# Latent queries projected in the first stage of a two-layer encoder kernel, and the latent values made beside the last band pair

## The chip, the cores and the metric

The kernel runs on one core of one Trainium2 chip. The metric is the device time of one launch in microseconds (us). TensorE (PE) does the matmuls, VectorE (DVE), ScalarE (ACT) and GpSimd (POOL) the rest, and SyncE (SP) issues nearly all transfers (DMAs).

## What is computed

Two layers of a streaming encoder, for 1024 prompt frames and 64 frames of a later chunk (1088 columns in all, with 256 cached positions). The first ("even") layer has two groups of eight heads beside each other: multi-head latent attention and chunk-band attention. The second layer is a stick-breaking attention. The change lies in the even layer alone:

```python
def _even_project(x, pos, w_in, g_q, w_uq, g_kv):
    h = x @ w_in
    q_a = (_rms_norm(h[..., :o1], g_q) @ w_uq).reshape(B, S, H_A, NOPE_DIM + ROPE_DIM)
    q_a = jnp.concatenate([q_a[..., :NOPE_DIM], _rope(q_a[..., NOPE_DIM:], pos)], -1)
    ckv = _rms_norm(h[..., o1:o2], g_kv)
    kr = _rope(h[..., o2:o3], pos)
    ...
def _mla_keys(ckv, kr, w_ukv):
    kv = (ckv @ w_ukv).reshape(B, T, H_A, NOPE_DIM + V_DIM)
    k = jnp.concatenate([kv[..., :NOPE_DIM], jnp.broadcast_to(kr[:, :, None, :], (B, T, H_A, ROPE_DIM))], -1)
    return k, kv[..., NOPE_DIM:]
def _even_prompt(x, pos, w_in, g_q, w_uq, g_kv, w_ukv, table, w_out):
    q_a, ckv, kr, q_b, k_b, v_b = _even_project(x, pos, w_in, g_q, w_uq, g_kv)
    k_a, v_a = _mla_keys(ckv, kr, w_ukv)
    o_a = _blockwise(lambda qb, pb: _softmax_attend(qb, k_a, v_a, _chunk_mask(pb, pos), MLA_SCALE), q_a, pos)
    o_b = _band_prompt(q_b, k_b, v_b, table)
    y = jnp.concatenate([o_a.reshape(B, S, H_A * V_DIM), o_b.reshape(B, S, H_B * HEAD_DIM)], -1) @ w_out
```

The query latent has 768 features, the key latent 256, and the rotated part of a query 32 features a head.

## The kernel before

All numbers are float32. A product is made from three matmuls: `split` (line 147) writes a high part H (ScalarE copies to a rounded type) and a low part L (VectorE subtracts), and `mm3` or `dense` (line 450) adds H.H, H.L and L.H in PSUM. PSUM has two buffers each of the tags d and s, three of t and one of pv.

The even layer runs in stages. `latents` (line 320) loads x and the weights and projects, tile by tile of 128 tokens, first the key latents (ck, and the rotated key kr), then the query latents; both are normed, transposed and stored raw to DRAM (`ck_d`, `krT_d`, `qn_d`). It also writes constant rows of the queries (qconst) to `qr_d`. Then `even_mixer` (line 745) works through four band pairs, two heads a pair: `proj` makes keys, queries and values of a pair, `attend` (line 729) its attention. For each row block: scores in PSUM, a maximum with the bias on VectorE (R, mx), exp on ScalarE, a reciprocal and a scaling on GpSimd, transposes on TensorE, a split of the transposed weights (wtH, wtL), the PV matmuls, and `put_output` (line 657), which folds two halves of the result (o; in latent attention through a second buffer, otmp, on GpSimd).

`paced` (line 558) spreads the steps of the next projection over the attention of the pair before, so the matmuls of the two are interleaved; the marks that it is given say behind which attention matmul a step may stand. Pairs 0 to 2 carry the projection of the next band pair in that way. Band pair 3 carries the query projection: `load_latents` (line 779) loads the query latents back from `qn_d` (six loads, 3.3 MB) and splits them, and does the same with ck; `rotate` (line 831, three chunks, weight blocks m = 4, 5) and `nope` (line 825, m = 0 to 3, three chunks each) project them and store the parts to `qr_d` and `qm_d`. What of it is not done when pair 3 ends runs behind it alone.

Then come the 11 value blocks (V, in two tiles of 6 and 2 heads), the latent keys of pair 0 (`proj_mla`, line 898, which also loads the queries of a pair from `qr_d` and `qm_d` and the weights w_mk), and four pairs of latent attention, each beside the keys of the next. Two key sets alternate; the constant rows of the second are copied from the first (k0H to k1L).

The order on each engine is that of the program after this pacing; a transfer waits in SP's queue for its buffer and for its place there, and each transfer takes one of eight completion lanes in turn, so it also waits until the eighth transfer before it has landed.

Of the kernel before, what the change touches and what calls it, by code (L numbers as in the profile page):

```python
# [7 lines left out]
F32 = mybir.dt.float32  # L8
# [111 lines left out]
class Net:  # L120
# [58 lines left out]
    def weight(self, src, shape, mark=None):  # L179
        nc = self.nc  # L180
# [4 lines left out]
        self.after(nc.sync.dma_start(tiles[0], src), mark)  # L185
# [134 lines left out]
    def latents(self):  # L320
        nc, io = self.nc, self.io
        pa = self.pool("pa", "right")
        wckH = self.tl(pa, [P, KD, LAT], "wckH", 1, F32R)
        wckL = self.tl(pa, [P, KD, LAT], "wckL", 1, F32R)
        wqlH = self.tl(pa, [P, KD, QL], "wqlH", 1, F32R)
        wqlL = self.tl(pa, [P, KD, QL], "wqlL", 1, F32R)

        def ck_piece(k):
            raw = self.tl(pa, [P, 2, LAT], "praw", 2)
            nc.sync.dma_start(raw, io["w_ck"][:, k : k + 2, :])  # L330
            self.split(wckH[:, k : k + 2, :], wckL[:, k : k + 2, :], raw)

        def ql_piece(k):
            raw = self.tl(pa, [P, QL], "praw", 2)
# [5 lines left out]
        def x_piece(t):  # L340
            t0, n = TOK[t]
            s = (slice(None), slice(None), slice(t0, t0 + n))
            raw = self.tl(pa, [P, KD, P], "xraw", 2)[:, :, :n]
# [28 lines left out]
        rope = self.tl(pa, [P, 9, ROPE], "rope", 1)  # L372
        nc.sync.dma_start(rope, io["rope_tok"])
        gkv = self.bcast(pa, io["g_kv"], CKV, "gkv")
        gq = None

        for t, (t0, n) in enumerate(TOK):
# [5 lines left out]
            sq = self.tl(pa, [P, 384], "sq", 2)  # L383
            ss = self.tl(pa, [P, 2], "ss", 3)
            nc.scalar.activation(sq[:n, :CKV], ps[:n, :CKV], AF.Square, accum_out=ss[:n, 0:1])
            kr = self.tl(pa, [P, ROPE], "kr", 2)
            nc.scalar.activation(kr[:n], ps[:n, CKV:LAT], AF.Copy)
            r = self.rstd(pa, ss[:n, 0:1], 1.0 / CKV, 1e-6, n)
            cat = self.tl(pa, [P, LAT], "cat", 2)
            nc.vector.scalar_tensor_tensor(cat[:n, :CKV], ps[:n, :CKV], r[:n], gkv[:n], op0=ALU.mult, op1=ALU.mult)  # L390
            cos, sin = rope[:n, t, :16], rope[:n, t, 16:]
            m = self.tl(pa, [P, 4, 16], "ropem", 2)
# [12 lines left out]
            stg = self.tl(pa, [P, 3, P], "stg", 3)  # L405
            nc.scalar.activation(stg[:, :2, :n], tp[:, :2, :n], AF.Copy)
            nc.scalar.activation(stg[:ROPE, 2, :n], tp[:ROPE, 2, :n], AF.Copy)
            nc.sync.dma_start(self.ck_d[:, :, t0 : t0 + n], stg[:, :2, :n])
            nc.sync.dma_start(self.krT_d[:, t0 : t0 + n], stg[:ROPE, 2, :n])

        gq = self.bcast(pa, io["g_q"], QL, "gq", marks[5])
        for t, (t0, n) in enumerate(TOK):
            if t == 4:
                first = self.weight(io["w_bk"][0], [P, KD, P], marks[-1])
            halves = []
            ss = self.tl(pa, [P, 2], "ss", 3)
            for h in range(2):
                ps = project(t, (wqlH, wqlL), h * 384, 384)
                sq = self.tl(pa, [P, 384], "sq", 2)
# [9 lines left out]
            for h in range(2):  # L429
# [4 lines left out]
                stg = self.tl(pa, [P, 3, P], "stg", 3)  # L434
                nc.scalar.activation(stg[:, :, :n], tp[:, :, :n], AF.Copy)
                nc.sync.dma_start(self.qn_d[:, 3 * h : 3 * h + 3, t0 : t0 + n], stg[:, :, :n])

        for c0, n in CHUNKS:
            qc = self.tl(pa, [ROPE, 384], "qc", 1)
            self.after(nc.sync.dma_start(qc[:, :n], io["qconst"][:, c0 : c0 + n]), marks[10])  # L440
            x = self.parts(pa, qc[:, :n], 2)
# [4 lines left out]
        pa.release()  # L446
        return first, marks[14]
# [209 lines left out]
    def put_output(self, cp, pv, width):  # L657
# [3 lines left out]
        if self.pool_fold:  # L661
            tmp = self.tl(self.pool_fold, [64, 256], "otmp", 2)
# [82 lines left out]
    def even_mixer(self):  # L745
# [30 lines left out]
        qnH = qnL = ckH = ckL = lc = kp0 = lq = up = None  # L776
        ksets = []

        def load_latents():


            nonlocal qnH, qnL, ckH, ckL, lc, kp0, lq, up
            X.release()
            lc = self.pool("lc", "left")
            kp0 = self.pool("kp0", "left")
            lq = self.pool("lq", "left")
            up = self.pool("uq", "left")
            qnH, qnL = (self.tl(lq, [P, KQ, T], tag, 1, F32R) for tag in ("qnH", "qnL"))
            ckH, ckL = (self.tl(lc, [P, 2, NK], tag, 1, F32R) for tag in ("ckH", "ckL"))

            def piece(H, L, src, n):
                raw = self.tl(up, [P, 2, 384], "raw", 3)
                nc.sync.dma_start(raw[:, :, :n], src)
                self.split(H, L, raw[:, :, :n])

            for c0, n in CHUNKS:
# [23 lines left out]
        def uq(ps, m, c0, n):  # L820
            if m not in uw:
                uw[m] = self.weight(io["w_uq"][m], [P, KQ, P])
# [937 lines left out]
```

## Time and profile before

| | |
|---|---|
| median of 3 runs | 2847.84 us (2845.25 to 2851.31) |
| profiled execution | 2850.05 us |
| its span on the core | 2848.3 us, 46969 instructions |
| mean granted clock of TensorE | 0.985 of full speed |

The span starts with the first instruction; the 1.75 us beside it in the execution's own time lie around it. The views read below are the page's header, windows (busy time of each engine in a stretch, with the clock granted to TensorE and the share and rate of the DMA engines), the chain of waits, which follows the work that ended last back from wait to wait, timelines and groups by form. `x12` is a count. An engine that waits for something is idle there, and the arrow names the releaser that came last.

### The profile page before, as it was taken

The page shows a single profiled execution, that of the slowest core. Times are in us where ns is not written, and L with a number is a line of the kernel's source. Part 1 is how long each engine was busy: PE and PEld are TensorE (multiplying, and loading weights), DVE is VectorE, ACT ScalarE, POOL GpSimd, SP SyncE. Part 2 cuts the span into 40 slices and gives each one's busy share as a digit, 9 for nine tenths or more (in the row PEclk, how much of TensorE's full clock was granted, in tenths as well). Part 3 has the DMA queues.
Part 4 walks back from the last instruction along what each step waited for, and adds up shares of the span by engine and source line. Part 5 has one row for each costly group of instructions (what it writes and reads, how often), then busy time and mean ns, then how long its engine had stood idle before and what let it go on. Part 6 is the DMA issues. An engine that isn't in the chain of part 4 may idle for free.

```text
span 2848.3 us, 46969 instructions
## 1 busy us (share of the span) xinstructions
PE 2742.8 (96%) x16907; PEld 2506.5 (88%) x16907; DVE 2158.1 (76%) x3822; ACT 1521.4 (53%) x3128; POOL 779.3 (27%) x891
## 2 busy tenths in 40 slices
PE   8999979999999999999999999999999999999998
PEld 7999978887899998878789999998879999977886
DVE  4256774885867777999967888888787777689998
ACT  4366654883555556333257777777445555543331
POOL 3223241662200002221543334344330000122235
PEclk9999999999999999999999999999999999999999
DMA  7322245334243447344321111112242444654432
GB/s 199 104 62 67 83 124 147 83 116 131 90 145 128 151 156 265 120 144 135 104 86 57 52 51 59 51 53 97 70 151 86 152 147 132 234 173 136 157 116 83
DMA packets 233320, 334.49 MB, mean 117 GB/s; under 512 B 45152, under 2 KB 165760, under 8 KB 233088
## 3 DMA queue, kind: packets, MB, share of 16 engines
q1 hardware_dynamic: 233088, 331.49, 37.1%
q8 instruction: 134, 2.20, 0.3%
q14 instruction: 98, 0.80, 0.1%
HBM read 216.72 MB, written 112.21 MB: 115 GB/s over the span
## 4 chain that ended last, share of the span: by engine, by line
PE 74%; DVE 10%; DMA 5%; ACT 5%; issue 3%; POOL 1%; SPq 1%; DVEq 0%; ACTq 0%; POOLq 0%
PE d L153 8%; PE d L154 8%; PE d L155 8%; PE t L153 5%; PE t L154 5%; PE t L155 5%; PE s L153 5%; PE s L155 5%; PE s L154 5%; PE t L171 4%; PE s L572 3%; PE pv L706 2%; PE pv L704 2%; PE pv L153 2%; PE pv L155 2%
## 5 line engine op out<-in xcount | busy, mean ns | idle before, releaser
L640 POOL TENSOR_TENSOR G<-G,S 128x384 f32<-128x384 f32 (+4 forms) x200 | 208.7, 1048 | 339.6 <-DVE S L637 139.8
L153 PE MATMUL d<-xH,wH 128*128 128x384 f32 (+1 forms) x792 | 266.4, 336 | 1.9 <-ACT kraw L539 1.4
L154 PE MATMUL d<-xL,wH 128*128 128x384 f32 (+1 forms) x792 | 264.3, 334 | 0.0
L155 PE MATMUL d<-xH,wL 128*128 128x384 f32 (+1 forms) x792 | 262.5, 331 | 0.0
L149 DVE TENSOR_TENSOR wtL<-t,wtH 128x512 fp32r<-128x512 f32 (+2 forms) x328 | 196.8, 618 | 46.9 <-ACT wtH L148 43.3
L148 ACT ACTIVATE wtH<-t 128x512 fp32r<-128x512 f32 (+2 forms) x328 | 170.3, 545 | 54.1 <-PE t L171 33.9
L148 ACT ACTIVATE wo<-wo 128x1024 fp32r<-128x1024 f32 (+4 forms) x109 | 96.1, 888 | 157.0 <-DMA wo<-a_d 27.1
L579 POOL TENSOR_TENSOR R<-R,inv 128x640 f32<-128x640 f32 (+6 forms) x100 | 120.4, 1212 | 199.7 <-DVE inv L578 87.5
L704 PE MATMUL pv<-wtH,V 128*128 128x256 f32 (+1 forms) x624 | 160.4, 281 | 8.5 <-ACT o L664 3.7
L706 PE MATMUL pv<-wtL,V 128*128 128x256 f32 (+1 forms) x624 | 156.8, 291 | 5.5 <-DVE wtL L149 5.3
L153 PEld LDWEIGHTS d<-xH,wH 128*128 128x128 f32 x792 | 149.7, 189 | 5.5 <-ACT kraw L539 2.2
L637 DVE TENSOR_TENSOR_SCAN S<-S,own 128x513 f32<-128x513 f32 (+3 forms) x144 | 144.2, 1010 | 11.4 <-ACT S L630 9.8
L154 PEld LDWEIGHTS d<-xL,wH 128*128 128x128 f32 x792 | 149.8, 189 | 1.2
L155 PEld LDWEIGHTS d<-xH,wL 128*128 128x128 f32 x792 | 149.7, 189 | 1.2
L704 PEld LDWEIGHTS pv<-wtH,V 128*128 128x128 f32 x624 | 120.7, 193 | 14.3 <-ACT o L664 6.3
L706 PEld LDWEIGHTS pv<-wtL,V 128*128 128x128 f32 x624 | 120.8, 194 | 8.9 <-DVE wtL L149 7.8
L171 PE MATMUL t<-ident,G 128*128 128x128 f32 x600 | 106.9, 282 | 14.3 <-POOL G L640 8.2
L572 PE MATMUL s<-kS,qH 128*128 128x384 f32 (+3 forms) x288 | 106.6, 373 | 6.9 <-DVE mx L595 4.1
L149 DVE TENSOR_TENSOR wo<-wo,wo 128x1024 fp32r<-128x1024 f32 (+4 forms) x80 | 92.9, 1165 | 21.9 <-ACT wo L148 20.9
L630 ACT ACTIVATE S<-s 128x384 f32<-128x384 f32 (+4 forms) x200 | 99.0, 495 | 12.6 <-PE s L572 9.1
L631 ACT ACTIVATE G<-s 128x384 f32<-128x384 f32 (+4 forms) x200 | 100.1, 500 | 0.0
L572 PE MATMUL s<-kS,qL 128*128 128x384 f32 (+3 forms) x288 | 97.8, 342 | 0.0
(1714 smaller groups left out, 9841.1 us busy)
## 6 DMA issues: line engine op xcount, KB each, us to landing
wo<-a_d SPq DMA_DIRECT2D x59, 512.0 KB, 3.8
wo<-in_w_dn SPq DMA_DIRECT2D x30, 512.0 KB, 5.5
a_d<-wo SPq DMA_DIRECT2D x27, 544.0 KB, 3.7
a_d<-sl SPq DMA_DIRECT2D x23, 544.0 KB, 4.0
sl<-in_w_up SPq DMA_DIRECT2D x22, 512.0 KB, 4.5
sl<-a_d SPq DMA_DIRECT2D x21, 512.0 KB, 3.8
sl<-in_w_dn SPq DMA_DIRECT2D x19, 512.0 KB, 5.3
xs<-a_d SPq DMA_DIRECT2D x19, 512.0 KB, 3.7
```

The costliest lines, as they stand in the source:

```text
L148: self.nc.scalar.activation(H, src, AF.Copy)
L149: (engine or self.nc.vector).tensor_tensor(L, src, H.bitcast(F32), op=ALU.subtract)
L153: i = mm(out, aH, bH, start=first, stop=False)
L154: mm(out, aH, bL, start=False, stop=False)
L155: mm(out, aL, bH, start=False, stop=last)
L171: return self.nc.tensor.transpose(out, in_, self.ident[:n, :n])
L572: self.nc.tensor.matmul(ps[:, :n], q, k, start=i == 0, stop=i == len(passes) - 1)
L579: nc.gpsimd.tensor_tensor(R[:, :nk], R[:, :nk], inv.to_broadcast([P, nk]), op=ALU.mult)
L637: nc.vector.tensor_tensor_scan(s[r], s[r], own, carry, op0=ALU.mult, op1=ALU.max)
L640: nc.gpsimd.tensor_tensor(G[:, :n], G[:, :n], S[:, 1 : n + 1], op=ALU.mult)
L704: mm(out, v, wH[:, s : s + n], start=bi == 0 and s == 0, stop=False)
L706: mm(out, v, wL[:, s - n : s], start=False, stop=bi == len(banks) - 1 and j == bank[-1][0])
```

## The change

The query latents are no longer stored: `latents` splits them into tiles in SBUF (`qn_parts`), and a new stage `queries` behind it projects and rotates them there and stores `qr_d` and `qm_d`; the qconst rows follow. The key latents are stored as H and L, and band pair 3 loads them so. w_mv and all four w_mk are loaded once, ahead of pair 3. The value blocks 0 to 7 are paced beside pair 3, and blocks 8 to 10 stand with the first latent keys; V is one tile of eight heads, whose last two are copied to a second tile by a transfer. The ring otmp has one buffer in place of two, and the ring of the staged ck tiles two in place of three.

```diff
@@ latents
-            stg = self.tl(pa, [P, 3, P], "stg", 3)
-            nc.scalar.activation(stg[:, :2, :n], tp[:, :2, :n], AF.Copy)
-            nc.scalar.activation(stg[:ROPE, 2, :n], tp[:ROPE, 2, :n], AF.Copy)
-            nc.sync.dma_start(self.ck_d[:, :, t0 : t0 + n], stg[:, :2, :n])
-            nc.sync.dma_start(self.krT_d[:, t0 : t0 + n], stg[:ROPE, 2, :n])
+            parts = [self.tl(pb, [P, 2, P], f"stg{x}", 2, F32R)[:, :, :n] for x in "HL"]
+            self.split(*parts, tp[:, :2, :n])
+            for i in range(2):
+                nc.sync.dma_start(self.ck_d[i, :, :, t0 : t0 + n], parts[i].bitcast(F32))
+            kr = self.tl(pb, [ROPE, P], "krT", 2)
...
+            if t in (2, 4):
+                uw[t // 2 + 3] = self.weight(io["w_uq"][t // 2 + 3], [P, KQ, P], marks[-1])
...
-                stg = self.tl(pa, [P, 3, P], "stg", 3)
-                nc.scalar.activation(stg[:, :, :n], tp[:, :, :n], AF.Copy)
-                nc.sync.dma_start(self.qn_d[:, 3 * h : 3 * h + 3, t0 : t0 + n], stg[:, :, :n])
+                c = slice(t0 - t // 3 * 384, t0 - t // 3 * 384 + n)
+                self.split(*(x[:, 3 * h : 3 * h + 3, c] for x in qn_parts[t // 3]), tp[:, :, :n])
+        pa.release()
+        late, first = self.queries(qn_parts, uw)
@@ queries (new; nope and rotate as before, on qn_parts)
+            ps = self.ps("ds")
+            first = uq(ps, m, c, n)
+            nc.sync.dma_start(self.qm_d[m, :, :, c0 : c0 + n], self.parts(up, ps[:, :n], 4))
...
+        for c in range(3):
+            rotate(c)
+        late = None
+        for m in range(4):
+            for c in range(3):
+                i = nope(m, c)
+                late = late or i
+            if m == 0:
+                first = self.weight(io["w_bk"][0], [P, KD, P], late)
@@ put_output
-            tmp = self.tl(self.pool_fold, [64, 256], "otmp", 2)
+            tmp = self.tl(self.pool_fold, [64, 256], "otmp", 1)
@@ load_latents
-            for c0, n in CHUNKS:
-                for k in range(0, KQ, 3):
...
-                    nc.sync.dma_start(raw, self.qn_d[s])
-                    self.split(qnH[s], qnL[s], raw, nc.gpsimd if c0 >= 768 else None)
+            for c0, n in ((0, 384), (384, 384), (768, 256), (SEQ, 64)):
+                kc = c0 if c0 < SEQ else SEQ + PAST
+                for i, x in enumerate((ckH, ckL)):
+                    nc.sync.dma_start(x[:, :, kc : kc + n].bitcast(F32), self.ck_d[i, :, :, c0 : c0 + n])
...
+            wv = self.weight(io["w_mv"], [P, 2, 512])
...
+            mk = self.weight([io["w_mk"][m] for m in range(4)], [P, KD, P])
@@ even_mixer
-        uqs = [lambda a=a: rotate(*a) for a in CHUNKS] + [lambda a=a: nope(*a) for a in ((m, c0, n) for m in range(4) for c0, n in CHUNKS)]
-        self.paced(uqs, marks[1:])
+        vals = [lambda j=j: values(j) for j in range(len(KEYBLK))]
+        self.paced(vals[:8], marks[1:])
...
-        Vs = [self.tl(vps[i], [P, 11, m, P], "V", 1, F32R) for i, m in enumerate((6, 2))]
...
-            w = self.weight(io["w_mk"][pair], [P, 2, P])
...
-        self.paced(steps, None)
+        self.paced(steps + vals[8:], None)
+        Vs.append(self.tl(vb, [P, 11, 2, P], "V", 1, F32R))
+        nc.sync.dma_start(Vs[1].bitcast(F32), Vs[0][:, :, 6:].bitcast(F32))
```

The order shows it at three places. On TensorE at the end of the last band pair, before: the last passes of the latent keys (d from ckH and the weight) stand ahead of the first latent scores (from k0H and q).

```order
L153 MATMUL d_5726<-ckH_4434,wH_1233_5698 128x512
L154 MATMUL d_5726<-ckL_4435,wH_1233_5698 128x512
L155 MATMUL d_5726<-ckH_4434,wL_1234_5699 128x512
L572 MATMUL d_5752<-k0H_4454,q_5705 128x384
L572 MATMUL d_5752<-k0L_4455,q_5705 128x384
L572 MATMUL d_5752<-k0H_4454,q_5705 128x384
L572 MATMUL s_5757<-k0H_4454,q_5705 128x512
```

After: the last PV passes of band pair 3 (pv) stand there instead.

```order
L774 MATMUL pv_5536<-wtH_5554,V_1939 128x256
L776 MATMUL pv_5536<-wtL_5555,V_1939 128x256
L774 MATMUL pv_5536<-wtH_5554,V_1939 128x128
L776 MATMUL pv_5536<-wtL_5555,V_1939 128x128
L642 MATMUL s_5736<-k0H_4985,q_5660 128x384
L642 MATMUL s_5736<-k0L_4986,q_5660 128x384
L642 MATMUL s_5736<-k0H_4985,q_5660 128x384
L642 MATMUL d_5741<-k0H_4985,q_5660 128x512
```

The latent keys and values have moved ahead of the last PV, and the first latent score has no matmuls between it and the band pair. On SP at the same place, before: the last of the four key copies (k1L) is followed by stores of the query projection (qm_d), two weight loads, more such stores and then the queries.

```order
L885 DMA k1L_5561<-k1L_4457 64x1344
L828 DMA qm_d<-raw_5365 256x1x384
L185 DMA wraw_5570<-in_w_mv 128x1024
L828 DMA qm_d<-raw_5388 256x1x320
L828 DMA qm_d<-raw_5417 256x1x384
L828 DMA qm_d<-raw_5440 256x1x384
L185 DMA wraw_5697<-in_w_mk 128x256
```

After: the copy of V, the key copies and the query loads (q, qS) stand close behind each other.

```order
L1063 DMA wH_2102_8409<-in_w_out 128x1024
L970 DMA V_5730<-V_5011 128x11x256
L779 DMA oT_d<-o_5430 64x256
L779 DMA oT_d<-o_5506 64x256
L932 DMA k0H_5650<-k0H_4985 64x1344
L932 DMA k0L_5651<-k0L_4986 64x1344
L779 DMA oT_d<-o_5562 64x256
L932 DMA k1H_5652<-k1H_4987 64x1344
L932 DMA k1L_5653<-k1L_4988 64x1344
L943 DMA q_5660<-qr_d 64x2x1024
L944 DMA qS_5658<-qr_d 64x2x64
L943 DMA q_5660<-qm_d 64x2x1024
```

Nothing of the query projection is left in between. On VectorE early in pair 3, before: splits of the loaded query latents (qnL) stand between the maxima (R, mx).

```order
L578 RECIPROCAL inv_4599<-sm_4597 128x1
L599 TENSOR_SCALAR nm_4629<-mx_4620 128x1
L149 TENSOR_TENSOR qnL_4433<-qnL_4433,qnH_4432 128x3x384 x2
L578 RECIPROCAL inv_4633<-sm_4631 128x1
L595 ISA R_4636,mx_4637<-s_4638,bias_4404 128x256
L595 ISA mx_4637 128x1
L149 TENSOR_TENSOR qnL_4433<-qnL_4433,qnH_4432 128x3x384
```

After: band values (V from t) and the first latent value block (V from d, 8 heads of 64) stand there.

```order
L149 TENSOR_TENSOR V_1939<-t_4929,V_1939 128x4x64
L648 RECIPROCAL inv_5036<-sm_5034 128x1
L669 TENSOR_SCALAR nm_5049<-mx_5040 128x1
L669 TENSOR_SCALAR nm_5104<-mx_5099 128x1
L149 TENSOR_TENSOR V_1939<-t_4929,V_1939 64x2x64
L149 TENSOR_TENSOR V_5011<-d_5566,V_5011 128x8x64
L665 ISA R_5111,mx_5112<-s_5113,bias_4942 128x256
L665 ISA mx_5112 128x1
```

The query latents' splits are gone from this stretch, and a value split has come in.

## Rows read from the trace of the kernel before

**Rows 1.** the page's busy times: us, share of the span, instructions of each engine.
```profile
PE 2742.8 (96%) x16907; PEld 2506.5 (88%) x16907; DVE 2158.1 (76%) x3822; ACT 1521.4 (53%) x3128; POOL 779.3 (27%) x891
```

**Rows 2.** windows of 20 us: PE, PEld, DVE, ACT, POOL busy; PEclk, DMA, GB/s.
```profile
200.00:220.00 20.00, 20.00 (x141) 19.80 (x140) 11.86 (x43) 13.64 (x35) 9.49 (x12) 1.00 0.26 76
...
380.00:400.00 20.00, 16.42 (x109) 15.81 (x109) 18.29 (x52) 10.58 (x25) 9.70 (x9) 0.88 0.32 79
400.00:420.00 20.00, 14.63 (x85) 13.51 (x85) 10.29 (x23) 8.66 (x20) 5.25 (x6) 0.91 0.34 100
...
480.00:500.00 20.00, 16.23 (x99) 15.10 (x100) 14.16 (x56) 12.34 (x30) 10.16 (x11) 0.83 0.07 16
500.00:520.00 20.00, 19.10 (x130) 17.27 (x130) 16.82 (x59) 17.15 (x41) 12.16 (x13) 1.00 0.65 148
```

**Rows 3.** chain of waits, 345 to 500 us: start, length, what.
```profile
351.93 9.69 DMA qnL<-qn_d
...
392.87 9.81 DMA qr_d<-raw
...
465.53 9.36 DMA q<-qm_d
474.94 6.57 DMA wraw<-in_w_mk
```

**Rows 4.** timeline of TensorE, 429 to 484 us: start, length, operation.
```profile
429.95 0.28 PE L706 MATMUL pv<-wtL,V 128*128 128x128 f32 x1
...
457.52 0.39 PE L153 MATMUL d<-wH,ckH 128*128 128x512 f32 x1
...
474.17 0.34 PE L572 MATMUL d<-k0H,q 128*128 128x384 f32 x1
...
483.14 0.48 PE L572 MATMUL d<-k1H,q 128*128 128x128 f32 x1 [5.73 <-DVE mx L612]
```

**Rows 5.** timeline of VectorE, 347 and 482 to 485 us.
```profile
347.57 0.41 DVE L595 CUSTOM_DVE_ANT_0 R<-s,bias 128x256 f32<-128x256 f32 x1
...
482.05 0.42 DVE L149 TENSOR_TENSOR wL<-wraw,wH 128x256 fp32r<-128x256 f32 x1 [5.99 <-ACT wH L148]
...
483.84 0.75 DVE L612 CUSTOM_DVE_ANT_0 R<-s,zero,mx 128x512 f32<-128x512 f32 x1
...
484.52 0.75 DVE L612 CUSTOM_DVE_ANT_0 R<-s,zero,mx 128x512 f32<-128x512 f32 x1
```

**Rows 6.** timeline of TensorE in the query projection, 441 to 444 us.
```profile
441.29 0.33 PE L154 MATMUL d<-qnL,wH 128*128 128x384 f32 x1
...
443.20 0.31 PE L153 MATMUL d<-qnH,wH 128*128 128x320 f32 x1
...
444.36 0.31 PE L155 MATMUL d<-qnH,wL 128*128 128x320 f32 x1
```

**Rows 7.** VectorE by form, 160 to 500 us: busy, mean ns, idle before.
```profile
L149 DVE TENSOR_TENSOR wtL<-t,wtH 128x512 fp32r<-128x512 f32 x44 | 29.3, 682 | 9.9 <-ACT wtH L148 9.5
L595 DVE CUSTOM_DVE_ANT_0 R<-s,bias,mx 128x384 f32<-128x384 f32 x32 | 19.5, 609 | 5.7 <-PE s L572 5.3
...
L668 DVE TENSOR_TENSOR o<-pv,o 64x256 f32<-64x256 f32 x32 | 13.1, 409 | 3.2 <-ACT o L667 2.9
...
L149 DVE TENSOR_TENSOR raw<-d,raw 128x384 fp32r<-128x384 f32 x8 | 4.4, 556 | 19.7 <-ACT raw L148 19.7
```

**Rows 8.** chain of waits, 20 to 65 us.
```profile
35.87 3.92 DMA krT_d<-stg
...
42.10 3.48 DMA ck_d<-stg
```

**Rows 9.** windows of 5 us, columns as in rows 2.
```profile
440.00:445.00 5.00, 5.00 (x33) 5.00 (x32) 1.12 (x2) 0.98 (x2) 0.00 (x0) 1.00 0.89 283
465.00:470.00 5.00, 5.00 (x23) 4.13 (x22) 3.06 (x8) 2.71 (x8) 0.00 (x0) 1.00 1.07 206
```

**Rows 10.** groups by form, 480 to 640 us.
```profile
L665 POOL TENSOR_TENSOR o<-o,otmp 64x256 f32<-64x256 f32 x28 | 21.6, 772 | 26.0 <-issue 14.6 <-ACT o L664 9.2 <-POOL Rs L579 1.5
```

More of the change, by code (lines that the diff above doesn't have):

```diff
@@ L184, in weight @@
                  for tag, dt in (("wraw", F32), (f"wH{self.wturn}", F32R), (f"wL{self.wturn}", F32R))]
-        self.after(nc.sync.dma_start(tiles[0], src), mark)
+        srcs = src if isinstance(src, list) else [src]
+        m = shape[1] // len(srcs)
+        for i, x in enumerate(srcs):
+            self.after(nc.sync.dma_start(tiles[0][:, i * m : i * m + m], x), mark)
         self.split(tiles[1], tiles[2], tiles[0])
@@ L438, in latents @@
         for c0, n in CHUNKS:
[L439 to L441 removed]
+            qc = self.tl(up, [ROPE, 384], "qc", 2)
+            self.after(nc.sync.dma_start(qc[:, :n], io["qconst"][:, c0 : c0 + n]), late)
+            x = self.parts(up, qc[:, :n], 4)
             for i in range(2):
@@ new lines, in load_latents, with values @@
+            Vs.append(self.tl(vp, [P, 11, 8, P], "V", 1, F32R))
+            nc.gpsimd.memset(Vs[0][DEC:, 10].bitcast(F32), 0.0)
+            mk = self.weight([io["w_mk"][m] for m in range(4)], [P, KD, P])
+            mk = [x.rearrange("p (m a) b -> p m a b", m=4) for x in mk]
+        def values(j):
+            c0, n = KEYBLK[j]
+            ps = self.ps("d")
+            first = None
+            for k in range(2):
+                i = self.mm3(ps[:n], ckH[:, k, c0 : c0 + n], ckL[:, k, c0 : c0 + n], wv[0][:, k, :], wv[1][:, k, :], k == 0, k == 1)
+                first = first or i
+            self.split(Vs[0][:n, j, :, :64], Vs[0][:n, j, :, 64:], ps[:n].rearrange("p (h d) -> p h d", h=8))
+            return first
@@ new lines, in mla_keys, with step @@
+        def mla_keys(pair):
+            tiles, w = ksets[pair % 2], [x[:, pair] for x in mk]
+            def step(c0, n):
+                ps = self.ps("ds")
+                first = self.dense(ps[:, :n], w, (ckH, ckL), 2, c0, n)
+                for e in range(2):
+                    h = slice(e * 64, e * 64 + 64)
+                    self.split(tiles[e][0][h, c0 : c0 + n], tiles[e][1][h, c0 : c0 + n], ps[h, :n])
+                return first
+            return [lambda a=a: step(*a) for a in ((0, 512), (512, 512), (SEQ, 320))]
@@ L877, in even_mixer @@
         up.release()
-        lq.release()
-        vps = [self.pool("mva", "left"), self.pool("mvb", "right")]
+        vb = self.pool("mvb", "right")
+        vps = [vp, vb]
         kp1 = self.pool("kp1", "right")
```

156 lines of the change are left out of this document (69 added, 87 removed).

## Prediction

> **What bounds the kernel now.** I read the page's header first, then the windows of 20 us, then the chain of waits of the stretch that the change touches, and last the timelines and the forms there. TensorE is busy 96% of the span [rows 1], but the windows show that this does not hold everywhere: in 380:400 it is busy 16.4 of 20 us at a granted clock of 0.88, in 400:420 only 14.6 at 0.91, in 480:500 16.2 at 0.83, where a dense window as 200:220 has 20.0 at 1.00 [rows 2]. The weak windows are the last band pair, with the query projection beside it, and the start of latent attention. The chain there does not run through matmuls: its longest pieces are transfers, 9.69 us of a qn load, 9.81 us of a qr store, 9.36 us of a query load and 6.57 us of a w_mk load [rows 3]. So the end is set by TensorE where it is dense, and between some 348 and 483 us by loads, stores and the two eviction engines around it. The change moves work out of that stretch into one where TensorE is dense.
>
> **Marks in the trace.** The first maximum of pair 3 starts on VectorE at 347.57 [rows 5]. The last PV pass of pair 3 is at 429.95, the query projection ends at 457.52, the first latent score is at 474.17, and the first score of the second head at 483.14 [rows 4]. From the first mark to the last it is 135.6 us.
>
> **Part 1, the query projection moves.** It is 18 groups of 18 passes, 12 groups of 384 columns and 6 of 320, so 216 and 108 passes. In a dense stretch eleven passes of 384 take from 441.29 to 443.20, 0.1736 us each, and eight of 320 from 443.20 to 444.36, 0.145 us each [rows 6]: 216 x 0.1736 + 108 x 0.145 = 53.2 us. In the first stage it stands between the query latents and the first band projection, all of it dense, so I charge it in full. Its evictions are hidden: a group takes 3.1 us of TensorE and one split of 128x384 0.56 us of VectorE [rows 7]; four staging buffers give a store some 12 us before its buffer is wanted, more than the 9.81 us above. The order puts the qconst copies between the last query eviction and the first evictions of the band projection on ScalarE and VectorE; the first matmul group that needs those done stands some 20 us of TensorE later, so they cost nothing; without that cover they would cost one load and its stores, up to the same 9.81 us.
>
> **Part 2, staging in the first stage.** 18 qn stores go; the ck stores double (9 more transfers in the first 60 us) and their ring shrinks from three tiles to two. The chain there already shows such stores as waits of 3.92 and 3.48 us [rows 8]. I take half of one more such wait, +2, bounds 0 and 6.
>
> **Part 3, pair 3 with the values beside it.** TensorE loses the filler: its passes from the first score to the last PV, with the 11 value blocks and the first latent keys, come to some 40 us by their columns at the price of [rows 6], so it is no longer the limit. VectorE is. By the order it has, from the first maximum to the last output fold: 19 splits of transposed weights (10 of 512, 5 of 384, 4 of 256 columns, 11.2 us), 24 maxima (12.1) with their reads, 17 reciprocals and 17 negations (7.0), 10 output folds (4.0), 11 value splits at the 512-column price of 0.682 (7.5), and by width the band values, raw and latent keys, cached latents and one weight split (10.3): 52.1 us at means as in [rows 7]. Records overlap, since maxima of 0.75 us start 0.68 us apart [rows 5]; 0.07 us off each of some 105 that have another close behind leaves 44.8 us. How full can the engine be? In 380:400 VectorE was busy 18.29 of 20 us; in latent attention, 500:520, 16.82; in 480:500, with waits, 14.16 [rows 2]. That gives 49, 53.3 and 63 us. I take 54, from the middle row, because its chain (score, maximum, exp, scale, transpose, split, PV) is that of pair 3. Ck no longer needs splitting; its first 384 columns are two loads issued after the last matmul of the projection, and some 25 passes and several maxima stand ahead of the first value block, so I charge that wait at nothing; uncovered it is no more than the 9.69 us of the qn load, which stood in the same place.
>
> **Part 4, the seam between pair 3 and latent attention.** Before, the key copies went out at the last PV and the queries were loaded behind the last qm store, both under 44 us of dense matmuls (429.95 to 474.17). Now nothing is left on TensorE to cover them: in the order the first latent score stands right behind the last PV, and SP's queue has the 1.44 MB copy of V, then four key copies (344 KB each, which wait for the last PV) and then the query loads (2.1 MB, with 0.13 MB for qS), and all stand in one queue. Price: in 465:470, when such loads ran, the DMA engines were full (1.07) at 206 GB/s [rows 9]. After the last PV that is 1.38 + 2.10 + 0.13 = 3.6 MB, 17.5 us; the V copy, 7.0 us at that rate, goes out with the last transposes, some 5 us before the last PV, and leaves 2 or 3; start and landing 2. Head 1 then has its queries 22 us after the last PV and head 0 about 16. Bounds: 15, if the V copy is done early and the rest runs at the 283 GB/s of 440:445 [rows 9]; 31, if the three batches follow each other with full landings (three times 9.36 us and the start [rows 3]). I take 22, since the 465:470 row is of these very loads.
> The Trainium skill, DMA: Bandwidth & Descriptors, section Anatomy of one DMA, gives 2.0 us plus bytes over 436 GB/s for one DMA, a fit of its software path. An estimate by it is 10 to 12 us for the seam in place of 22, and the sum would be about 2831. By that rule the trace does not agree: these loads filled the engines at less than half that rate.
>
> Credit: at 483.14 before, VectorE had stood 5.99 us behind a w_mk split and resumed at 482.05, so three of the four maxima of head 0 and one key split were still to do; afterwards they are done while head 1's queries land. Three starts 0.68 us apart and the reads make 2.4 us [rows 5].
>
> **Small parts.** One otmp buffer in place of two: ScalarE's copy must wait for GpSimd's add (0.77 us) of the row before; there are 28 in 160 us [rows 10], some 5 us apart, so it is mostly free: +1.5, bounds 0 and 3. Three w_mk splits leave latent attention (0.42 us as at 482.05): -0.8, net of overlap. The ring of sq and the earlier w_out loads cost nothing: ScalarE alone writes sq and nobody reads it, and no row of the chain waits for w_out.
>
> **Sum.** Late stretch: 54 + 22 = 76 in place of 135.6, less 2.4: -62.0. First stage: 53.2 + 2 = +55.2. Small: +0.7. Together -6.1 us. The profiled execution took 2850.05 us (span 2848.3) and the median of the runs shown is 2847.84, 0.08% apart; I take the difference from the median: 2842 us.
>
> **Rivals.**
> A, the forecast, 2842. Its own spread is 50 to 58 us for pair 3 and 19 to 25 for the seam: 2835 to 2849.
> B, a quicker seam and a fuller VectorE. If VectorE reaches its share of 380:400 (49 us) and the seam runs at 283 GB/s (3.6 MB in 12.7 us, with start and rest 17), it is 2842 - 5 - 5 = 2832. For it: both rates were reached. Against: the first beside a dense filler, the second not by query loads. The rate of the Trainium skill, DMA: Bandwidth & Descriptors, would end here too.
> C, no gain: pair 3 keeps to the share of a stretch with waits (63 us) and the seam is 20 us: 2849. For it: in-order engines without a filler stand on the longest latency, and every step of a row changes engine. Against: 500:520 holds 16.82 with the same steps.
> D, slower: the seam is a serial chain. V copy, key copies and query loads share one queue, and a load whose lane is taken goes out only when an earlier copy has landed, so that the batches line up with full landings, 31 us in place of 22. With pair 3 at a share of 0.75 (60 us) that is 2842 + 9 + 6 = 2857. It decides from a seam of 34 us with pair 3 at 54, or 28 with 60. For it: a query load took 9.36 us from issue to landing, where its own 0.5 MB is 2.5 us at 206 GB/s; against it: the loads overlapped there.
> That the change does not do what it says is settled by the order: all 18 groups stand ahead of the first band projection and all value blocks ahead of the last PV.
>
> **How the numbers follow.** A measurement of this kernel tells about 0.2%, 5.7 us, from no change. Chances: A 0.48, of which 0.27 lies below 2842.1 and 0.21 above; B 0.20; C 0.12; D, with the first stage's stores at their bound as another way there, 0.20. Faster 0.27 + 0.20 = 0.47, same 0.21 + 0.12 = 0.33, slower 0.20. The range leaves out half of D and the far end of B: 2829 to 2857.
>
> **What would show it.** In the profile after: 324 query passes in a row at 0.17 and 0.145 us ahead of the band projections, with no new waits on stores in the first 60 us; about 54 us from the first maximum of pair 3 to its last PV, with VectorE the fullest engine; then TensorE idle some 16 us, waiting for a query load, and head 1's scores at 22. The prediction is wrong if pair 3 takes over 60 us, if the seam is under 15 or over 30 us, or if the band pairs ahead of it move.

## The result, and the profile after

Measured beside the kernel before on the same chip, the changed kernel takes 2856.24 us (median of 15 runs) against 2847.11 (15 runs): ratio 1.0031 [1.0023, 1.0039], 9 us slower. The forecast was 2842, faster; the time lies inside the range, on the wrong side of no change.

The profiled execution of after took 2852.04 us (span 2850.3), 4 us under its median, and that of before 2850.05, 3 us over its own. So totals are compared by medians, and the two traces by distances between marks. Behind the last mark, the first w_out pass, the change alters next to nothing, and there the traces of this case differ by chance: 2216.7 us in before, 2212.7 in after, 2211.8 to 2222.7 over all runs. TensorE's row of after, against [rows 1] (us, share, instructions):

```profile
PE 2732.2 (96%) x16907; PEld 2497.7 (88%) x16907; DVE 2154.3 (76%) x3827; ACT 1511.9 (53%) x3104; POOL 767.9 (27%) x888
```

The marks of after, from the timeline of TensorE, as in [rows 4]: last PV of pair 3, first latent score, first score of the second head.

```profile
468.97 0.41 PE L776 MATMUL pv<-wtL,V 128*128 128x128 f32 x1
...
483.99 0.66 PE L642 MATMUL s<-k0H,q 128*128 128x384 f32 x1 [14.60 <-DMA q<-qm_d]
...
489.48 0.42 PE L642 MATMUL s<-k1H,q 128*128 128x128 f32 x1 [0.35 <-DMA q<-qm_d]
```

Distances between marks, in us:

| stretch | before | after | difference | forecast |
|---|---|---|---|---|
| start to the first band projection | 123.7 | 188.2 | +64.5 | +55.2 |
| to the first maximum of pair 3 | 223.9 | 222.6 | -1.2 | 0 |
| pair 3, first maximum to last PV | | 58.1 | | 54 |
| seam, last PV to head 1's first score | | 20.5 | | 22 |
| these two together | 135.6 | 78.6 | -57.0 | -59.6 |
| head 1's first score to the first w_out pass | 148.5 | 148.1 | -0.4 | -1.7 |
| sum at that pass | 631.6 | 637.6 | +6.0 | -6.1 |

Forecast and traces differ by 12 us at that pass (by 14 in the medians), and three quarters of it stand in one row, the first stage. Windows of after, columns as in [rows 2]: the whole query projection and the whole of pair 3, then four of 5 us in the query projection.

```profile
124.55:188.23 63.68, 57.32 (x337) 56.16 (x336) 27.30 (x44) 17.92 (x36) 10.13 (x10) 0.95 0.49 164
410.87:468.97 58.10, 48.65 (x293) 40.33 (x291) 44.51 (x136) 39.66 (x90) 17.86 (x21) 0.97 0.38 111
...
150.00:155.00 5.00, 5.00 (x34) 5.00 (x33) 0.00 (x0) 0.25 (x1) 0.00 (x0) 1.00 0.28 104
155.00:160.00 5.00, 0.64 (x4) 0.32 (x2) 2.90 (x4) 2.51 (x5) 0.00 (x0) 0.86 0.57 183
160.00:165.00 5.00, 4.12 (x13) 4.12 (x14) 1.11 (x2) 0.76 (x3) 0.00 (x0) 0.50 0.27 102
165.00:170.00 5.00, 4.01 (x25) 3.75 (x23) 1.64 (x2) 1.47 (x2) 0.00 (x0) 0.95 0.85 261
```

TensorE is idle 6.4 of 63.7 us, 5.2 of them in one stall that ends at 160.9; behind it, in 160:165, the granted clock is 0.50, the lower level of 1.2 GHz. Where the stores of the rotated queries run with little beside them (150:155, 160:165) the DMA engines are busy 0.27 or 0.28 and move 102 to 104 GB/s; in 165:170 they are busy 0.85 and move 261. The waits in 118:200 (us in total, times, longest) and the chain of waits (start, length, what):

```profile
ACT wH L148 <- DMA wraw<-in_w_bk: 10.0, 1, 10.0
ACT raw L148 <- DMA qr_d<-raw: 8.7, 3, 3.4
PE s L153 <- DVE raw L149: 6.4, 2, 5.2
```

```profile
145.06 9.67 DMA wraw<-in_w_bk
154.75 1.07 ACT wH L148
...
158.13 10.88 DMA qr_d<-raw
```

ScalarE works in order. It stands on the split of the weight w_bk, whose load shares SP's queue with the stores, and then on staging buffers that the stores hold. So the evictions of PSUM stop, and TensorE waits for a buffer there (the third wait: a pass into s, released by the split of raw).

### The profile page after: what moved, and what is told of

Its sections match the earlier page's. It is cut to its first block, busy times and chain, and to the rows that moved or that the text cites. A ratio compares the mean times of both kernels' runs of the same rounds, so it can differ in the third digit from the quotient of the medians.

```text
span 2850.3 us, 46910 instructions
## 1 busy us (share of the span) xinstructions
PE 2732.2 (96%) x16907; PEld 2497.7 (88%) x16907; DVE 2154.3 (76%) x3827; ACT 1511.9 (53%) x3104; POOL 767.9 (27%) x888
## 4 chain that ended last, share of the span: by engine, by line
PE 74%; DVE 10%; ACT 5%; DMA 4%; issue 4%; POOL 2%; SPq 1%; DVEq 0%; ACTq 0%; POOLq 0%
PE d L153 9%; PE d L154 8%; PE d L155 8%; PE t L153 5%; PE t L155 5%; PE t L154 5%; PE s L153 5%; PE s L155 5%; PE s L154 5%; PE t L171 4%; PE s L642 3%; PE pv L776 2%; PE pv L774 2%; PE pv L155 2%; PE pv L153 2%
## 5 line engine op out<-in xcount | busy, mean ns | idle before, releaser
L149 DVE TENSOR_TENSOR wtL<-t,wtH 128x512 fp32r<-128x512 f32 (+2 forms) x328 | 197.4, 619 | 54.4 <-ACT wtH L148 43.5
L774 PE MATMUL pv<-wtH,V 128*128 128x256 f32 (+1 forms) x624 | 159.7, 282 | 9.7 <-DVE o L738 6.6
L153 PEld LDWEIGHTS d<-xH,wH 128*128 128x128 f32 x784 | 148.2, 189 | 6.6 <-ACT qS L599 3.2
L155 PEld LDWEIGHTS d<-xH,wL 128*128 128x128 f32 x784 | 148.1, 189 | 1.2
L154 PEld LDWEIGHTS d<-xL,wH 128*128 128x128 f32 x784 | 148.1, 189 | 1.1
L774 PEld LDWEIGHTS pv<-wtH,V 128*128 128x128 f32 x624 | 120.6, 193 | 14.0 <-DVE o L738 5.7
```

Source lines behind the costliest of these rows:

```text
L149: (engine or self.nc.vector).tensor_tensor(L, src, H.bitcast(F32), op=ALU.subtract)
L153: i = mm(out, aH, bH, start=first, stop=False)
L154: mm(out, aH, bL, start=False, stop=False)
L155: mm(out, aL, bH, start=False, stop=last)
L774: mm(out, v, wH[:, s : s + n], start=bi == 0 and s == 0, stop=False)
```

## Experiments

Ratios are against the kernel before on the same chip, with 95% intervals; the changed kernel's is 1.0031. "Stage" is the distance from the first query pass to the first band projection, 63.7 us in after.

### What stops the query stage

**e1**, the w_bk weight two groups later; **e2**, rotated parts in a ring of four buffers of their own (and the ring of u weights, those of the groups without rotation, cut to two to make room); **e3**, each store cut into four of 16 partitions.

```diff
 e1: -            if m == 0:
     +            if m == 2:
                      first = self.weight(io["w_bk"][0], [P, KD, P], i)
 e2: +                x = self.parts(up, r, 4, "rraw")
     +                uw[m] = [self.tl(up, [P, KQ, P], f"u{m % 2}{x}", 1, F32R) for x in "HL"]
 e3: +                    for e in range(4):
     +                        nc.sync.dma_start(self.qr_d[e, base + 16 * i : base + 16 * i + 16, :, c0 : c0 + n], x[o * 64 + 16 * e : o * 64 + 16 * e + 16])
```

> The changed kernel with one edit: the first w_bk weight is loaded and split behind the query groups of m = 2 instead of m = 0. In the changed kernel the query stage took 63.8 us from its first to its last matmul (53.2 forecast), with a TensorE stall of 5.25 us at 160.9. Theory S (ScalarE stands in order behind the w_bk split, whose load landed 9.7 us after issue): the stall goes, the stage takes 54 to 57 us, the whole is 6 to 9 us shorter than the changed kernel, about level with the kernel before. Theory Q (the four staging buffers are held by qr_d stores, which are slow): the evictions still wait for qr_d, a stall of 3 us or more stays, the stage takes 59 us or more, the whole gains at most 3 us.

> The changed kernel with a staging ring of four of its own for the rotated parts (room for it is made by two weight sets in place of four for the unrotated groups); w_bk stays where it is. Theory S: ScalarE still waits some 8 to 10 us for w_bk ahead of the first unrotated evictions, a stall of 4 us or more stays, gain under 2 us. Theory Q: no eviction waits for a qr_d store any more and the stall falls under 2 us, the stage takes 54 to 57 us, gain 6 to 9 us.

> The changed kernel with each qr_d store of 64 partitions cut in four of 16 partitions, one a head pair; nothing else. If the old form runs on few of the 16 DMA engines (share 0.2 and about 100 GB/s in the windows where only these stores run), the new form moves the same bytes in well under half the time, no eviction waits for qr_d, w_bk lands in 5 us, and the stage takes 54 to 57 us: gain 6 to 9 us. If the rate is that of the queue and not of the form, the windows stay at about 100 GB/s; then 36 more transfers of about 0.6 us of issue each make SP late and the stage stays at 60 us or more.

e1: 2859.34, 1.0031 [1.0018, 1.0044], stage 62.1. The stall stays at 5.2 us, and another weight stands where w_bk stood:

```profile
ACT raw L148 <- DMA qr_d<-raw: 12.0, 4, 3.2
ACT u3H L148 <- DMA uraw<-in_w_uq: 10.2, 1, 10.2
```

So it is not that weight; it is whatever is queued with the stores. e2: 2861.41, 1.0041 [1.0027, 1.0056], stage 66.5, with stalls of 7.6 us: the ring alone doesn't help, for ScalarE then stands 16.0 us on the weight w_bq in the same queue (and the smaller u ring took something away, so it is no clean test). e3: 2870.54, 1.0081 [1.0061, 1.0101], stage 67.1: SP spent 31.14 us on the 48 issues, 0.65 us each, the share rose to 0.43 only and the rate fell to 78 GB/s. A piece is 49 KB (16 x 2 x 384 x 4 bytes), and one in 0.65 us is 75 GB/s, so SP's issue is enough to explain e3's rate, and e3 leaves open whether the form of the old stores was slow. Its window:

```profile
155.00:160.00 5.00, 0.87 (x3) 0.80 (x3) 0.56 (x1) 0.49 (x1) 0.00 (x0) 0.92 0.43 78
```

### The same stores in another row order

qr_d was [pair, row]: 64 partitions of SBUF went to 4 pairs of 16 rows. In **e6** it is [row, pair], and the weights' columns and the cos and sin rows are laid out so that the 64 partitions are 64 rows that lie behind each other. Bytes and pieces stay as in after, and by operation and tile so does the order on every engine. The layout of the constant rows' stores and of the query loads follows. **e7** leaves the stores as they are and begins with groups that need no rotation, with their weights loaded ahead in place of the rotated ones'.

```diff
 e6: -        self.qr_d = tc.dram_tile([4, P, 2, T], F32, name="qr_d")
     +        self.qr_d = tc.dram_tile([P, 4, 2, T], F32, name="qr_d")
     -        self.qr_d[:, base + 16 * i : base + 16 * i + 16, :, c0 : c0 + n]
     +        self.qr_d[base + 16 * i : base + 16 * i + 16, :, :, c0 : c0 + n].rearrange("r e i t -> (r e) i t")
 e7: -        for c in range(3):
     -            rotate(c)
         for m in range(4):
             for c in range(3):
                 i = nope(m, c)
     +                if m == 2:
     +                    rotate(c)
```

> The changed kernel, except that the rotated queries are stored with the rows ahead of the pairs (a store's 64 partitions then lie one behind the other as 64 rows of the destination, where they were 4 pairs of 16 rows; the columns of the two weights and the rows of cos and sin are laid out to match). Twelve stores, the same bytes and the same pieces as before. Theory Q (the stores themselves are slow, since each occupies about a quarter of the DMA engines, share 0.27 at 102 GB/s, and so the staging ring and the loads queued behind them come late): the share in stretches with these stores alone rises above 0.6, a store lands in under 5 us in place of 8 to 11, ScalarE's waits on them (8.7 us in all) mostly go, the stall of 5.2 us at 160.9 goes; the query stage takes 54 to 57 us in place of 63.8 and the kernel 2847 to 2850. Theory W (the weight splits stand badly in ScalarE's order, whatever the stores do): the stall stays at 4 us or more, the stage at 61 to 64, the kernel at 2854 to 2857.

> The changed kernel, except that the query stage begins with the groups 0 and 1, which need no rotation and whose stores lie over all rows, and the three rotations stand between the groups of m = 2; the weights that are loaded ahead are those of m = 0 and 1. The stores are the old ones (4 pairs of 16 rows). Theory Q (slow stores hold up whatever is queued behind them): the weights of the stage are now loaded ahead of the slow stores, and their staging buffers are wanted late; no stall of over 2 us in the stage, 54 to 58 us in place of 63.8, kernel 2847 to 2852; but the first band projections may meet the tail of the stores. Theory W (weight splits in ScalarE's order ahead of evictions): the splits of u2, u4 and w_bk now stand behind the second eviction, TensorE stalls there for 3 us or more, and the stage stays over 60 us, the kernel at 2853 to 2858.

e6: 2850.01, 1.0005 [0.9991, 1.0019]; stage 54.4, no stall. Its windows and its waits, and then SP's timeline of after and of e6 (start, length, issues):

```profile
150.00:155.00 5.00, 5.00 (x32) 5.00 (x31) 2.74 (x6) 2.08 (x4) 0.00 (x0) 1.00 0.86 270
160.00:165.00 5.00, 5.00 (x32) 5.00 (x31) 1.05 (x2) 0.93 (x2) 0.00 (x0) 1.00 0.65 240
```

```profile
ACT wH L148 <- DMA wraw<-in_w_bk: 3.4, 1, 3.4
...
ACT raw L148 <- DMA qr_d<-raw: 1.6, 3, 0.7
```

```profile
148.24 6.35 SPq L497 DMA_DIRECT2D qr_d<-raw  x4
...
157.55 5.79 SPq L497 DMA_DIRECT2D qr_d<-raw  x4
```

```profile
145.13 2.78 SPq L497 DMA_DIRECT2D qr_d<-raw  x4
...
150.30 2.51 SPq L497 DMA_DIRECT2D qr_d<-raw  x4
```

The row order of the stores takes the stall and 9.2 us of the stage away; SP is through four of them in 2.5 to 2.8 us where it took 5.8 and 6.4 (4.2 for the first four). The Trainium skill, DMA: Bandwidth & Descriptors, section Why a DMA increments its semaphore by 16 and not by 1, says that a DMA runs on the largest number of engines, at most 16, that divides the slowest dimension of both its sides, which for 4 pairs is four of 16; the share of 0.27 agrees with that, and by the same rule 64 rows get all. e7: 2858.32, 1.0032 [1.0021, 1.0043]. Its stage is 54.5 as well, as theory Q said, but its total is that of after: the slow stores now stand ahead of the first band projections' cached keys, and from the first band projection to the first maximum of pair 3 it takes 232.2 us where after has 222.6, with TensorE waiting up to 4.1 us for ScalarE's copies of these keys (kraw). Moving slow stores moves their price.

**e10** is e6 with the constant rows copied from their input in the first stage, 6 transfers in place of 12 stores behind the query projection.

> Rows ahead of pairs in the stored rotated queries (as in the run before this that had only this), and the constant rows of the stored queries are copied straight from their input in the first stage, 6 transfers in place of 3 loads, 3 splits and 12 stores behind the query projection (their H part is 0 or 1 and equal to the input, their L part is 0). Theory: of the 9.3 us that the rows gave back in the query stage 2 to 3 were lost again in the first band projections, where ScalarE waited 7.6 us for a constant and then 3.1 us for the cached keys behind twelve stores that SP issued at some 0.9 us each, until TensorE waited for PSUM; without them the way from the first band projection to the first score takes 37 us in place of 38.7 and TensorE's waits for the staged keys (1.5 and 0.8 us) go: 2847 to 2849. Rival (the band pairs differ by chance from run to run): no change against rows alone, 2850.

In e6 2.7 of the 9.2 us are lost again behind the stage: from the first band projection to the first maximum of pair 3 it takes 225.3 us where after has 222.6, and TensorE waits 1.5 and 0.8 us there for ScalarE's copies of the cached keys. e10: 2849.68, 1.0005 [0.9996, 1.0015], the time of e6. Those waits are gone and the stretch takes 222.7 us. But the six transfers now stand ahead of the load of the norm weights gq; VectorE waits 5.9 us for these, TensorE 2.0, and the granted clock is 0.91 over 60:80:

```profile
60.00:80.00 20.00, 18.04 (x98) 17.49 (x98) 7.17 (x15) 4.44 (x11) 1.09 (x2) 0.91 0.16 48
```

The first query pass is at 127.75 in e10 and at 123.91 in e6 (123.91 to 125.93 in the runs that leave the first stage ahead of it alone). So e10 moves this price as e7 moved the other, and does not show that the constants cost nothing.

### The values and the seam

**e5** puts the copy of V behind the third PV group of the first latent pair. **e8** holds all value blocks until the last row of pair 3 is transposed, which takes back the second half of the change. **e11** is e8 with the w_out loads later. **e15** is e6 with e5 and six of the eleven blocks held, **e14** e6 with e5.

```diff
 e5:  -        nc.sync.dma_start(Vs[1].bitcast(F32), Vs[0][:, :, 6:].bitcast(F32))
      +            if pair == 0:
      +                self.after(nc.sync.dma_start(Vs[1].bitcast(F32), Vs[0][:, :, 6:].bitcast(F32)), marks[2])
 e8:  -        self.paced(vals[:8], marks[1:])
      -        self.paced(steps + vals[8:], None)
      +        self.paced(steps, None)
      +        self.paced(vals, [marks[-1]], 0)
 e11: +            self.after(nc.sync.dma_start(raw, w[k * P : (k + 1) * P, :]), mark)
```

> The changed kernel with the copy of the two last heads' values issued during the first latent pair instead of ahead of the key copies. In the changed kernel the first latent score came 15.0 us after the last band PV and head 1's 20.5 us after. If the copy still holds the queue when the last PV ends, the two shorten by 2 to 4 us (11 to 13 and 17 to 18) and the whole by 1 to 4 us. If key copies and query loads alone set them, they stay within 1 us and so does the whole.

> The changed kernel, except that all 11 value blocks of the latent layer are held until the last row of band pair 3 is transposed, so that most of them stand behind the last PV, where TensorE waited 15 us for the first queries; this takes back the second half of the change alone. Theory V (beside pair 3 the values cost VectorE and ScalarE time that the seam has free): pair 3 loses 8 splits of 0.68 us, 58.1 goes to 52 to 55 us; the 11 blocks of 6 passes of 512 columns, some 15 us, lie under the query loads; first score of the second head as long after the last PV as now (20.5), TensorE's wait there under 5 us and its clock 0.9 and more; kernel 2849 to 2853. Theory R (the seam is set by VectorE and by the loads, and the values only move): pair 3 gets shorter by as much as the first scores come later, and the kernel stays at 2854 to 2858.

> The values held until the last row of band pair 3 (as in the run before this that had only this), and the first loads of the output weights wait for the fifth PV group of the first latent pair. Theory: in the run without the second edit pair 3 did give 7 us, and they were lost again because the first output weight, whose buffer is the one of w_mv, came free only with the values, was loaded behind six query loads, and ScalarE stood on it until 487.9 with the first exponentials of the latent layer behind it; TensorE lost 2.5 us in 490 to 495 and the rows behind it more. With the load out of the way the stretch from the first score of the second head to the first output projection takes 148 to 150 us in place of 154.0, and the kernel 2849 to 2852. Rival (latent attention is longer since its rows meet the rest of the query loads, whatever ScalarE does): it stays at 152 us or more and the kernel at 2854 to 2857.

> As the run beside it, with five value blocks beside pair 3 and six held until the last row of pair 3 is transposed. Theory (VectorE beside pair 3 is freed, but latent attention loses as much to a lower granted clock and more idle time of TensorE as soon as matmuls fill the seam): pair 3 takes 54 to 56 us in place of 58.1, the stretch from the first score of the second head to the first output projection 150 to 156 in place of 148, and the kernel 2848 to 2854, no better than the run beside it. Rival (the loss came from the late release of the w_mv buffer or from all eleven blocks at once): that stretch stays at 148 to 149 and the kernel falls to 2844 to 2847.

| run | ratio | pair 3 | seam | head 1's first score to w_out |
|---|---|---|---|---|
| after | 1.0031 [1.0023, 1.0039] | 58.1 | 20.5 | 148.1 |
| e6 | 1.0005 [0.9991, 1.0019] | 58.0 | 20.7 | 148.9 |
| e5 | 1.0024 [1.0014, 1.0033] | 58.6 | 20.6 | 148.0 |
| e8 | 1.0025 [1.0014, 1.0036] | 51.0 | 20.2 | 154.0 |
| e11 | 1.0042 [1.0027, 1.0058] | 51.1 | 21.2 | 157.4 |
| e14 | 1.0001 [0.9991, 1.0012] | 58.0 | 20.4 | 148.2 |
| e15 | 1.0021 [1.0011, 1.0031] | 53.7 | 20.4 | 155.6 |

In e5 the wait of TensorE in the seam is the same as in after, so the copy of V doesn't set it:

```profile
PE s L642 <- DMA q<-qm_d: 15.0, 2, 14.7
```

e14 (2848.64 us) can't be told from e6 by its ratio.

The values do cost pair 3 some 7 us, a little more than theory V said, but latent attention takes 6 to 9 us longer once they are gone from there. So e8's total (2855.51 us) is that of theory R, by a loss that neither theory named. In e8's chain behind the seam stands the load of w_out, and I took that for the cause:

```profile
480.48 7.01 DMA wH<-in_w_out
```

e11 takes it out of the way, and the loss grows. So that load there is not needed for the loss; but e11 is no clean test, for its later loads run in latent attention (in 510:520 the DMA share is 0.57), and what they add is not known. Windows of e11, and below of after, at a row of latent attention:

```profile
510.00:520.00 10.00, 7.92 (x35) 6.89 (x34) 6.42 (x16) 9.01 (x22) 5.59 (x6) 0.66 0.57 121
```

```profile
540.00:550.00 10.00, 8.76 (x60) 7.87 (x60) 7.47 (x35) 7.61 (x20) 5.68 (x6) 1.00 0.10 19
```

Both kernels have short stalls there (idle 2.1 and 1.2 of 10 us); in e11 the mean granted clock is 0.66, in after 1.00. TensorE runs the same work in the stretch, 931 to 935 matmuls in each of the four kernels. Windows of 5 us from the one mark to the other give its idle time and the busy time lost to the clock, (1 - granted) times busy: 10.9 and 2.7 us in after, 13.6 and 4.1 in e8, 12.9 and 9.1 in e11, 14.0 and 7.3 in e15. That is 4.1 us more than after in e8 (of 5.9 lost), 8.4 in e11 (of 9.3), 7.7 in e15 (of 7.6). So idle time and clock carry most of the loss in e8 and nearly all of it in the others, and e15 (2853.49 us) came out as its theory said; why the clock falls behind one stall and not behind another, no run here settles.

**e9** (e6, e7 and e8 together) and **e12** (e10 and e11 together) took 2850.51, 1.0006 [0.9995, 1.0016], and 2853.11, 1.0012 [1.0002, 1.0022]: no better than e6.

> The changed kernel with the three edits together: rows ahead of pairs in the stored rotated queries, the groups without rotation first, and the values held until the last row of pair 3. If the prices of the stage (some 9 us over the dense time, with its stall) and of the values beside pair 3 (4 to 6 us) both come back and are independent: 2856 - 8 - 5 = 2843, between 2840 and 2847, that is not slower than the kernel before the change. If only the stage comes back: 2847 to 2850; if neither: 2854 to 2858.

> All four edits: rows ahead of pairs, constants copied straight in the first stage, values held until the last row of pair 3, output weights later. If the prices add, 2856 - 6 (rows) - 2 (constants) - 5 (values and output weights): 2843, between 2840 and 2846, faster than the kernel before the change by some 0.15%. If the values give nothing: 2847 to 2849.

### The kernel before with the same row order

**e13** is the kernel before with e6's row order and nothing else; by operation and tile every engine has the order of before. **e16** is e13 with the w_mk weight of the next latent pair behind the second PV group.

```diff
 e16: -            w = self.weight(io["w_mk"][pair], [P, 2, P])
      +            w = self.weight(io["w_mk"][pair], [P, 2, P], mark)
      -                score, steps = proj_mla(pair + 1)
      +                score, steps = proj_mla(pair + 1, marks[1])
```

> The kernel before the change, except that its rotated queries are stored with the rows ahead of the pairs (same engines' orders, same bytes, same pieces). Theory P (the price of these stores is one of place: in the first stage the weights and buffers of a dense stretch wait behind them, while before the change the query projection stood beside band pair 3, which VectorE limits): pair 3 and the query projection end within 3 us of before, the kernel 2845 to 2849, no change. Rival G (the stores cost the same wherever they stand): the stretch from the first maximum of pair 3 to the first score of the second head falls from 135.6 to 127 to 130 us, the kernel 2839 to 2843.

> The kernel before the change with rows ahead of pairs in the stored rotated queries, and the w_mk weight of the next latent pair loaded only behind the second PV group of the pair before. In the run with the rows alone ScalarE waited 6.99 us for that weight (462 to 468.8) with a latent key split behind it, VectorE's maximum waited for that, and TensorE stood 6.1 us for VectorE before the second head's first score at 470.37. Theory (the wait is the latest thing there): that score starts 5 to 7 us earlier, the stretch behind it stays at 148, and the kernel takes 2826 to 2830. Rival (given back: latent attention meets a lower granted clock or later keys): 2831 to 2835.

e13: 2833.77, 0.9946 [0.9933, 0.996], 15 us faster than before. Theory P falls, and G holds by more than it said (127 to 130 us): from the first maximum of pair 3 to head 1's first score it takes 122.5 us in place of 135.6. All of it comes ahead of the last PV pass of pair 3, which stands at 416.82 in place of 429.95 (e13's timeline of TensorE):

```profile
416.82 0.28 PE L706 MATMUL pv<-wtL,V 128*128 128x128 f32 x1
```

Windows of e13, against [rows 2]:

```profile
380.00:400.00 20.00, 16.51 (x108) 15.88 (x107) 18.80 (x55) 12.81 (x31) 9.59 (x9) 0.87 0.37 95
400.00:420.00 20.00, 20.00 (x135) 19.90 (x135) 13.35 (x27) 9.90 (x23) 5.26 (x6) 1.00 0.68 205
420.00:440.00 20.00, 20.00 (x118) 19.49 (x117) 5.22 (x8) 4.53 (x8) 0.00 (x0) 1.00 0.76 226
```

In 400:440 TensorE is full, where before it was busy 14.6 of the first 20 us. The chain of before has two more pieces there, behind the 9.81 us of [rows 3], which are gone from e13's chain as that one is:

```profile
405.08 8.43 DMA wraw<-in_w_uq
...
417.58 6.59 DMA qr_d<-raw
```

From the last PV pass to head 1's first score it takes 53.6 us in e13, as in before (53.2). A wait for w_mk is left there, in e13's timeline (start, length, operation; idle before and its releaser):

```profile
468.83 0.42 ACT L148 ACTIVATE wH<-wraw 128x256 fp32r<-128x256 f32 x1 [6.99 <-DMA wraw<-in_w_mk]
...
470.37 0.47 PE L572 MATMUL d<-k1H,q 128*128 128x128 f32 x1 [6.08 <-DVE mx L612]
```

In e16 that stall is gone:

```profile
462.78 0.33 PE L572 MATMUL d<-k1H,q 128*128 128x128 f32 x1
```

Head 1 starts at 462.78, the stretch behind it takes 145.1, and e16 takes 2828.78, 0.9925 [0.991, 0.9941]: 21 us faster than before, and the fastest kernel here.

## Why the prediction was wrong

**Part 1 is the step that failed.** "Its evictions are hidden ... four staging buffers give a store some 12 us before its buffer is wanted, more than the 9.81 us above." The 9.81 us of [rows 3] was read as the latency of one store. It belonged to a group of twelve stores that keep the DMA engines busy to about a quarter (0.27) and hold SP's queue while they are issued, so it should have been read as a rate: twelve stores are 2.2 MB, at some 100 GB/s 22 us in which every load behind them is late. In place of 53.2 + 2 the first stage took 64.5: 54.4 of dense passes (e6; the 53.2 was 1.2 short), 6.4 idle, 2.9 of clock (busy 57.3 us in place of 54.4), the rest ahead of it. No rival named this. D had "the first stage's stores at their bound", but meant those of ck. Those cost no more than forecast: the first query pass came 0.85 us after the mark of before, and 0.2 to 2.2 us over the runs that leave that part alone, where +2 was forecast.

**The credit side of the same error.** The sum took all 135.6 us of the late stretch as work that the move frees. 13 of them were this wait, which travels with the stores and needed no move to go (e13). With fast stores on both sides the forecast's question has another answer: the move then costs 16 us (e6 at 1.0005 against e13 at 0.9946). By the marks of these two the late stretch shrinks by 43.8 us (122.5 to 78.8) and the first stage grows by 54.5: the query projection had filled TensorE beside pair 3, where it cost less than in a dense stage.

**Part 3, mechanism right, size off by 4.** VectorE was busy 44.51 us in pair 3, forecast 44.8. Its share was 0.77, not the 0.84 taken from 500:520: without a filler pair 3 waits more than latent attention, between the middle row and that of 480:500 (0.71). TensorE's largest wait there is 5.2 us for the output fold (PE pv L774 on DVE o L738).

**Part 4 was right**: 20.5 us to head 1 and 15.0 to head 0, forecast 22 and 16, DMA share 1.03 to 1.07 at 204 to 219 GB/s in 475:490. The two or three us for the copy of V were not there (e5); without them the forecast's own sum is 19.5. The estimate of 10 to 12 us worked out from the figure of the Trainium skill, DMA: Bandwidth & Descriptors, section Anatomy of one DMA, does not agree with this trace.

**Small parts.** The credit of 2.4 for latent attention hardly came: that stretch is 0.4 us shorter, forecast 1.7. The qconst copies were to "cost nothing": ScalarE waited 5.6 us for them, and TensorE 1.3 us for copies of the cached keys that stand behind them on ScalarE; e10 moved that price and didn't take it away. That the range (2829 to 2857) held the time was luck: its upper end came from a seam of 31 us (D), and the seam took 20.5.

## What to carry to other kernels

A transfer that lands late is first a rate: set its bytes over its time against what the DMA engines move elsewhere in the same trace, and look at the share; here a share of a quarter was the mark of a form that could be mended in place, by the order of the rows. Before work is moved to get rid of a wait, ask whether the wait travels with it; here the move kept it, and mending it where it stood was worth 15 us. Time saved in one stretch is a gain only when the next stretch, its clock included, keeps its length (e8: 7 us saved, 6 lost).

## What the runs showed of the hardware

- A store from 64 partitions to 4 pairs of 16 rows ran at a DMA share of 0.27 and some 102 GB/s; the same bytes to 64 rows in line at shares of 0.65 to 0.97, beside other transfers. SP needed 4.2 to 6.4 us to issue four of the one and 2.5 to 2.8 of the other.
- Each piece of a store cut into four took 0.65 us of SP's queue (31.14 us for 48), and at 49 KB a piece the rate came down to 78 GB/s.
- After a stall of 5.25 us TensorE was granted 0.50 in 160:165 (after). The same wait for ScalarE's output copy late in latent attention, 1.58 us in after and 1.59 in e6, was followed by a granted clock of 1.00 in after (599:604) and of 0.74 in e6 (592:597).
